# Second layer's attention: query projections in halves, output pieces one by one, each tied behind its step's scores

## The chip, the cores and the metric

The kernel runs on one core of one Trainium2 chip. The metric is the device time of one execution in microseconds (us). Its engines are TensorE (PE in the profile, with PEld for the loading of its weights), VectorE (DVE), ScalarE (ACT), GpSimd (POOL) and SyncE (SP), which here only issues transfers.

## The reference

A trunk of two layers over 512 latent tokens and 256 context tokens, 1024 wide. The change lies in the second layer's first half: grouped-query attention with 16 query heads, 4 key-value heads, head width 64, a window of 128 tokens either way, all context keys, and a learned sink logit per head. Cut to that part:

```python
def mixer_c(h_x, h_c, w_in, w_out, sinks, cos, sin, with_ctx_out):
    q_x, k_x, v_x = jnp.split(h_x @ w_in, [C_Q_COLS, C_Q_COLS + C_KV_COLS], axis=-1)
    q_x = apply_rope(heads(q_x, GQA_HEADS), cos, sin)
    k_x = apply_rope(heads(k_x, GQA_KV_HEADS), cos, sin)
    ...
    def blk(q_b, start):
        ...
        return gqa_sink_attend(q_b, jnp.concatenate([k_c, k_b], axis=1),
                               jnp.concatenate([v_c, v_b], axis=1),
                               jnp.concatenate([ctx_mask, band], axis=-1), sinks)
    out_x = block_sweep(blk, q_x).reshape(B, S, C_Q_COLS) @ w_out
```

Behind it come the gated residual, a norm, the feed-forward and the final norm.

## The kernel before

All arithmetic is in 32 bits. A projection splits both operands into a high and a low part and adds three products of them (`mm3`, L205 to L209: high by high, high by low, low by high), so a tile of 128 output columns by 512 tokens over 1024 inputs is 8 x 3 = 24 matmuls. Weights come through a stream `S`: SP loads a raw tile, ACT casts its high part (L158), DVE subtracts to get the low part (L159); `S.next()` hands out the next pair and makes two more ready ahead. The pools hold three of each.

The attention stage has eight query tiles `m` of two heads each. `q_piece(m)` projects one tile (24 matmuls into PSUM, tile `t` for the first and the single bank `lin` for the others) and calls `q_tile`: the rope (DVE shuffle L380 and product L381, which read the PSUM bank, then two POOL instructions L382 and L383), then ACT (L369) and DVE (L372) write the two halves of `gq`, of which there are four buffers.

There are 32 attention steps, `gqa_step(m, i)`, four per tile, one for each block of 128 queries. Each has two parts. Part `a` makes, for each of two heads, the scores in one of two PSUM buffers `s` (L1513 for the context keys, L1515 for the window; eight matmuls a step), adds the mask and takes the maximum on DVE (L1517), the exponential on ACT (L1522, L1524), the sum and reciprocal on DVE (L1526, L1527) and the scaling on POOL (L1530). Part `b` turns the probabilities by PE transposes (L1542, eight, and L1554, two in the steps with a longer window), copies them out on ACT and DVE (L1550, L1548, L1555), and in every second step makes the value products (L396, a block of twenty matmuls for two steps) and splits the result (L196, L197).

`run_steps` writes the steps out as: part `a` of step n, part `b` of step n - 1, then the fillers of step n. Fillers are projections for PE to do while a softmax is under way. A table `plan` gives them by tile: tiles 1 and 2 of the queries in tile 0's four steps, 3 and 4 in the next four, then one tile for each four steps, and from tile 5 on the eight pieces of `first_part`, the output projection's first half (`wo1` with `k0 = 0`: 12 matmuls over the heads of tiles 0 to 3, into `lin`, and a gated residual on DVE, L1591). The order written is not the order on the engines: a scheduler places each engine's instructions by its own estimate of when their inputs are ready, so it may draw fillers ahead of the step they were written in. Only `issue_after(x)` holds an instruction behind `x`, where both are on one engine.

Behind the 32 steps, the output projection's second half runs (`wo1` with `k0 = 4`), then the residual's norm and the feed-forward.

Of the kernel before, what the change touches and what calls it, by code (L numbers as in the profile page):

```python
# [15 lines left out]
P = 128  # L16
D = 1024
KT = D // P
NX = 512
NC = 256  # L20
# [17 lines left out]
def tile_trunk(  # L38
# [27 lines left out]
    nc = tc.nc  # L66
# [126 lines left out]
    S = Stream()  # L193
# [8 lines left out]
        nc.gpsimd.dma_start(f32(lo), src, accum_op=ALU.add)  # L202
        nc.scalar.copy(hi, src)

    def mm3(ps, wh, wl, xh, xl, n=KT):  # L205
        for k in range(n):
            nc.tensor.matmul(ps, wh(k), xh(k), start=k == 0, stop=False)  # L207
            nc.tensor.matmul(ps, wh(k), xl(k), start=False, stop=False)  # L208
            end = nc.tensor.matmul(ps, wl(k), xh(k), start=False, stop=k == n - 1)  # L209
        return end  # L210
# [17 lines left out]
    def wslice(t, m=P):  # L228
        v = t.rearrange("p (k m) -> p k m", m=m)
        return lambda k: v[:, k, :]  # L230
# [127 lines left out]
    xh = lambda k: hx[k][:, 0, :]  # L358
    xl = lambda k: hx[k][:, 1, :]
# [4 lines left out]
    def evac_pair(dst, col, n, src, scale):  # L364

        c = slice(col, col + n)
        for j in range(2):
            a = slice(64 * j, 64 * j + 64)
            nc.scalar.activation(dst[a, j, c], src[a, :], AF.Copy, scale=scale)  # L369
        for j in range(2):  # L370
            a, o = slice(64 * j, 64 * j + 64), slice(64 - 64 * j, 128 - 64 * j)
            nc.vector.scalar_tensor_tensor(  # L372
                dst[o, j, c], src[a, :], scale, f32(dst[a, j, c]), op0=ALU.mult, op1=ALU.subtract
            )
# [46 lines left out]
    def vload():  # L421
        return [tuple(wslice(t, 256) for t in S.next()) for _ in range(2)]

    def run_steps(steps, fillers):

        prev = None
        for n, (a, b) in enumerate(steps):
            a()
            if prev:
                prev()  # L430
            prev = b
            for f in fillers[n] if n < len(fillers) else []:
                f()
        prev()

    def spread(items, n):
        out_ = [[] for _ in range(n)]
        for i, f in enumerate(items):
            out_[i * n // len(items)].append(f)
        return out_  # L440
# [172 lines left out]
    with ExitStack() as st:  # L613
# [3 lines left out]
        linp = lambda: lin.tile([P, NX], F32, tag="lin", name="lin")  # L617
# [32 lines left out]
        with ExitStack() as s0:  # L650
# [7 lines left out]
            def ada0_mm(b):  # L658
                ps = tp()
                for k in range(KT):  # L660
                    ada_mm(ps, S.next(0), k, k == 0, k == KT - 1)
                    S.request(min(S.at + 8, 2 * KT + 3))
                return ps
# [8 lines left out]
            ps = ada0_mm(0)  # L672
# [381 lines left out]
        ps = linp().rearrange("p (t c) -> p t c", t=2)  # L1054
# [47 lines left out]
        def first_part(t):  # L1102
            def f():
                w = S.next()
                for m in (2 * t, 2 * t + 1):
                    wo_chunk(m, w, "x", 0)
                    wo_chunk(m, w, "c", 0)
            return f

        steps, fillers = [], []  # L1110
        for u in range(8):
# [23 lines left out]
            steps += us  # L1135
            fillers += spread(fl, len(us))
        run_steps(steps, fillers)
        prep(KT - 1)()


        held = []
        for t in range(4):
            w = S.next(3)
# [29 lines left out]
    with ExitStack() as st:  # L1173
# [17 lines left out]
        q_tile = lambda: fp.tile([P, 4 * H], F32, tag="q", name="q")  # L1191
# [234 lines left out]
    with ExitStack() as st:  # L1426
# [6 lines left out]
        linp = lambda: lin.tile([P, NX], F32, tag="lin", name="lin")  # L1433
# [11 lines left out]
        def q_tile(m, ps):  # L1445
            qs[m] = gp.tile([P, 2, NX], F32R, tag="gq", name="gq", bufs=4)
            evac_pair(qs[m], 0, NX, rope_of(ps, gp), -0.125)
# [33 lines left out]
        def q_piece(m):  # L1481
            def f():
                wh, wl = (wslice(t) for t in S.next())
                ps = linp() if m else tp()
                mm3(ps, wh, wl, xh, xl)
                q_tile(m, ps)
            return f

        def att(m):

            if m < 4:
                return hc[2 * m], hc[2 * m + 1]
            return [hx[m][:, i, :].rearrange("p (a n) -> p a n", a=2) for i in range(2)]
# [4 lines left out]
        def gqa_step(m, i):  # L1498
            kv = m // 2
            lo, hi = max(i - 1, 0), min(i + 1, 3)  # L1500
            nk = (hi - lo + 1) * P
            d = {}

            def a():
                q = qs[m]
                small = lambda name: gp.tile([P, 2], F32, tag=name, name=name, bufs=4)
                mx, rs, es = small("mx"), small("rs"), small("es")
                pp = []
                for c in range(2):
                    ql = q[:, c, i * P : (i + 1) * P]  # L1510
                    s = sps.tile([P, 1024], F32, tag="s", name="s")
                    for n, k in ((0, k1), (1, k2)):
                        nc.tensor.matmul(s[:, 256:512], ql, k[:, kv, 0:NC], start=(n == 0), stop=(n == 1))  # L1513
                    for n, k in ((0, k1), (1, k2)):
                        nc.tensor.matmul(s[:, 512 : 512 + nk], ql, k[:, kv, NC + lo * P : NC + lo * P + nk], start=(n == 0), stop=(n == 1))  # L1515
                    sv = s[:, 256 : 512 + nk]
                    nc.vector.tensor_tensor_reduce(  # L1517
                        out=sv, in0=sv, in1=gm0 if i == 0 else gm[:, 0 : 256 + nk], op0=ALU.add, op1=ALU.min,
                        scale=1.0, scalar=snk[:, 2 * m + c : 2 * m + c + 1], accum_out=mx[:, c : c + 1],
                    )  # L1520
                    p = gp.tile([P, 640], F32, tag="p", name="p", bufs=5)
                    nc.scalar.activation(p[:, 0 : 256 + nk], sv, AF.Exp, bias=mx[:, c : c + 1], scale=-1.0, accum_out=rs[:, c : c + 1])  # L1522
                    sk = 2 * m + c
                    nc.scalar.activation(es[:, c : c + 1], snk[:, sk : sk + 1], AF.Exp, bias=mx[:, c : c + 1], scale=-1.0)  # L1524
                    pp.append(p)
                nc.vector.tensor_add(rs, rs, es)  # L1526
                nc.vector.reciprocal(rs, rs)  # L1527
                for c in range(2):
                    z = pp[c][:, 0 : 256 + nk]
                    nc.gpsimd.tensor_scalar(z, z, rs[:, c : c + 1], 1.0, op0=ALU.mult, op1=ALU.mult)  # L1530
                d["p"] = pp
# [71 lines left out]
        for m in range(KT):  # L1603
# [2 lines left out]
        super_weights(1, type("", (), {"tile": lambda self, *a, **k: spool[0].tile(*a, **k)})())  # L1606
        q_piece(0)()
        steps, fillers = [], []
        plan = {
            0: [q_piece(1), q_piece(2)], 1: [q_piece(3), q_piece(4)], 2: [q_piece(5)], 3: [q_piece(6)], 4: [q_piece(7)],  # L1610
            5: first_part(0), 6: first_part(1) + first_part(2), 7: first_part(3),
        }
        for m in range(8):
            steps += [gqa_step(m, i) for i in range(4)]
            fillers += spread(plan[m], 4)
        run_steps(steps, fillers)
        held = []
        for t in range(4):
            w = S.next(0 if t >= 2 else 2)
# [336 lines left out]
```

## Time and profile before

| what | us |
|---|---|
| median of three runs | 1614.59 (1612.83 to 1619.76) |
| the profiled execution | 1613.67 |
| its span in the profile | 1611.6 |
| PE busy | 1538.8 (95%) |
| DVE busy | 1252.2 (78%) |
| ACT busy | 743.4 (46%) |
| POOL busy | 273.5 (17%) |
| first scores of the stage | at 1047.00 |
| last value products begin | at 1219.27 |

The span is counted from the profile's first instruction to its last; the execution's own time has 2.1 us around it. All places are given in us from the span's start. Matmuls overlap, so the time from the start of one to the start of the next is what one costs in a row, and not its own duration. PE being busy is no proof that it runs at full clock; the windows give the clock that was granted, 1.00 being full.

### The profile page before, as it was taken

Reading aid. Unit: us, or ns where it says so; the run is one execution under the profiler, and the core shown is the slowest. Engines: PE = TensorE matmul, PEld = TensorE weight load, DVE = VectorE, ACT = ScalarE, POOL = GpSimd, SP = SyncE. Lnnn points to the kernel's source line nnn. Section 1 sums busy time; section 2 is a strip of 40 time slices with the busy share of each in tenths; the row PEclk is TensorE's granted clock in tenths of the full one; section 3 lists DMA queues with packets and bytes.
Section 4 is the critical chain, followed back from the end, with each engine's and each line's share of the span. In section 5 each row is a group of like instructions: output and inputs, shape, how many; then the busy total and the mean of one; then the engine's idle time right before and its main releaser. Section 6 shows DMA issues by size and latency. Waiting matters only on the chain.

```text
span 1611.6 us, 25394 instructions
## 1 busy us (share of the span) xinstructions
PE 1538.8 (95%) x9774; PEld 1378.4 (86%) x9774; DVE 1252.2 (78%) x2141; ACT 743.4 (46%) x1292; POOL 273.5 (17%) x311
## 2 busy tenths in 40 slices
PE   5899999998999999999999999998999999999997
PEld 3798988787878999999999998886778899989897
DVE  4757789876698889869899777686766987868686
ACT  5445655455344523333424245466764543525344
POOL 2222214354010000010100001264332000000001
PEclk9999999999999999999999999999999999999999
DMA  9322255544145455575756752311011441323321
GB/s 347 103 62 77 78 160 163 180 152 117 57 144 144 119 165 155 150 197 159 206 171 164 211 155 83 107 56 38 14 40 46 138 144 66 131 68 104 118 79 53
DMA packets 69216, 198.41 MB, mean 123 GB/s; under 512 B 6900, under 2 KB 19348, under 8 KB 69096
## 3 DMA queue, kind: packets, MB, share of 16 engines
q1 hardware_dynamic: 59464, 164.40, 31.0%
q0 software_dynamic: 9056, 31.87, 9.4%
q8 instruction: 77, 1.26, 0.3%
q10 hardware_dynamic: 576, 0.52, 0.1%
q14 instruction: 43, 0.35, 0.1%
HBM read 160.45 MB, written 4.86 MB: 103 GB/s over the span
## 4 chain that ended last, share of the span: by engine, by line
PE 49%; DVE 10%; DMA 6%; issue 4%; ACT 1%; POOL 0%; DVEq 0%; POOLq 0%; ACTq 0%; SPq 0%
PE f L1737 4%; PE f L1736 4%; PE f L1735 4%; DMA wl<-raw 3%; PE f L208 3%; PE f L209 3%; PE f L207 3%; PE f L1307 2%; PE f L1305 2%; PE f L1306 2%; PE f L1788 2%; PE f L1789 2%; PE f L1790 2%; PE t L396 2%; DMA raw<-in_w_dram 2%
## 5 line engine op out<-in xcount | busy, mean ns | idle before, releaser
L196 ACT ACTIVATE wh<-raw 128x1024 fp32r<-128x1024 f32 (+1 forms) x96 | 92.2, 978 | 232.2 <-DVE raw L525 102.2
L207 PE MATMUL lin<-hb,wh 128*128 128x512 f32 (+1 forms) x456 | 161.6, 356 | 9.9 <-DVE k L372 4.2
L208 PE MATMUL lin<-hb,wh 128*128 128x512 f32 (+1 forms) x456 | 159.8, 351 | 0.2
L209 PE MATMUL lin<-hb,wl 128*128 128x512 f32 (+1 forms) x456 | 158.3, 347 | 0.0
L197 DVE TENSOR_TENSOR wl<-raw,wh 128x1024 fp32r<-128x1024 f32 (+1 forms) x96 | 107.2, 1122 | 36.4 <-ACT wh L196 34.5
L269 DVE SCALAR_TENSOR_TENSOR junk<-raw,tables 128x1024 bf16<-128x1024 f32 x80 | 98.9, 1237 | 19.0 <-DMA raw<-in_ada_wT_dram 18.6
L202 POOL DMA_DIRECT2D wl<-raw x39 | 34.1, 874 | 445.2 <-ACT wl L201 346.0
L207 PEld LDWEIGHTS lin<-hb,wh 128*128 128x128 f32 x456 | 86.5, 190 | 24.0 <-issue 5.7
L1346 PE MATMUL f<-g,wh 128*128 128x512 f32 (+1 forms) x304 | 102.8, 339 | 0.5 <-DVE s L1335 0.5
L1347 PE MATMUL f<-g,wh 128*128 128x512 f32 (+1 forms) x304 | 102.7, 339 | 0.0
L1736 PE MATMUL f<-hb,wh 128*128 128x256 f32 x360 | 101.7, 283 | 0.0
L1348 PE MATMUL f<-g,wl 128*128 128x256 f32 (+1 forms) x304 | 100.8, 336 | 0.9 <-DMA wl<-raw 0.9
L1735 PE MATMUL f<-hb,wh 128*128 128x256 f32 x360 | 101.4, 283 | 0.0
L1737 PE MATMUL f<-hb,wl 128*128 128x256 f32 x360 | 101.2, 283 | 0.0
L208 PEld LDWEIGHTS lin<-hb,wh 128*128 128x128 f32 x456 | 86.7, 190 | 11.4 <-issue 0.6
L1307 PE MATMUL f<-hb,wl 128*128 128x384 f32 x288 | 96.2, 334 | 0.0
L1305 PE MATMUL f<-hb,wh 128*128 128x384 f32 x288 | 96.2, 334 | 0.0
L1306 PE MATMUL f<-hb,wh 128*128 128x384 f32 x288 | 96.2, 334 | 0.0
L209 PEld LDWEIGHTS lin<-hb,wl 128*128 128x128 f32 x456 | 86.6, 190 | 10.7
L158 ACT CAST wh<-raw 128x1024 fp32r<-128x1024 f32 x61 | 63.9, 1047 | 66.6 <-PE lin L208 17.6
L159 DVE TENSOR_TENSOR wl<-raw,wh 128x1024 fp32r<-128x1024 f32 x61 | 79.1, 1297 | 18.0 <-ACT wh L158 17.6
L339 POOL TENSOR_TENSOR ns_a<-ns_a,ns_s 128x256 f32<-128x256 f32 (+1 forms) x16 | 18.7, 1169 | 430.9 <-ACT ns_s L335 424.3
(393 smaller groups left out, 4883.1 us busy)
## 6 DMA issues: line engine op xcount, KB each, us to landing
raw<-in_w_dram SPq DMA_DIRECT2D x132, 512.0 KB, 3.7
raw<-in_ada_wT_dram SPq DMA_DIRECT2D x80, 512.0 KB, 4.1
wl<-raw POOLq DMA_DIRECT2D x39, 512.0 KB, 6.5
raw<-in_w_ab_dram SPq DMA_DIRECT2D x24, 512.0 KB, 3.9
raw<-in_ada_w_dram SPq DMA_DIRECT2D x16, 512.0 KB, 9.4
k<-k SPq DMA_DIRECT2D x16, 384.0 KB, 5.1
raw<-in_w_c_dram SPq DMA_DIRECT2D x12, 512.0 KB, 3.9
nb<-in_na_bias_dram POOLq DMA_DIRECT2D x16, 256.0 KB, 3.4
```

The costliest lines, as they stand in the source:

```text
L197: return nc.vector.tensor_sub(lo, src, f32(hi))
L207: nc.tensor.matmul(ps, wh(k), xh(k), start=k == 0, stop=False)
L208: nc.tensor.matmul(ps, wh(k), xl(k), start=False, stop=False)
L209: end = nc.tensor.matmul(ps, wl(k), xh(k), start=False, stop=k == n - 1)
L1305: nc.tensor.matmul(ps, wh(k), b[:, 0, :], start=k == 0, stop=False)
L1306: nc.tensor.matmul(ps, wh(k), b[:, 1, :], start=False, stop=False)
L1307: nc.tensor.matmul(ps, wl(k), b[:, 0, :], start=False, stop=k == 3)
L1346: nc.tensor.matmul(ps, hi, g[:, 0, cols[v]], start=first, stop=False)
L1347: nc.tensor.matmul(ps, hi, g[:, 1, cols[v]], start=False, stop=False)
L1735: nc.tensor.matmul(ps, wh(k), b[:, 0, :], start=k == 0, stop=False)
L1736: nc.tensor.matmul(ps, wh(k), b[:, 1, :], start=False, stop=False)
L1737: nc.tensor.matmul(ps, wl(k), b[:, 0, :], start=False, stop=k == 3)
```

## The change

`q_piece` stays for tile 0 alone. Tiles 1 to 7 are projected by `q_halves(m)`: two fillers of 12 matmuls, the first over the inputs 0 to 3, the second over 4 to 7 into the same `lin` bank, with the rope behind the second. The table is gone. The 14 halves are spread over steps 0 to 16 (none in steps 5, 11 and 16), the eight output pieces over steps 17 to 31 (steps 17, 18, 20, 22, 24, 26, 28, 30). And each step's fillers are written inside `issue_after` on the last score matmul issued, `scored[0]`, which is that of the same step: a filler can no longer be drawn ahead of its step's scores.

```diff
-    def mm3(ps, wh, wl, xh, xl, n=KT):
-        for k in range(n):
+    def mm3(ps, wh, wl, xh, xl, n=KT, ks=None):
+        for k in ks or range(n):
...
-    def run_steps(steps, fillers):
+    def run_steps(steps, fillers, pin=None):
...
-            for f in fillers[n] if n < len(fillers) else []:
-                f()
+            with tc.issue_after(pin[0].ins) if pin else nullcontext():
+                for f in fillers[n] if n < len(fillers) else []:
+                    f()
...
+        def q_halves(m):
+            d = {}
+
+            def f(i):
+                if i == 0:
+                    d["w"] = [wslice(t) for t in S.next()]
+                    d["ps"] = linp()
+                mm3(d["ps"], *d["w"], xh, xl, ks=range(4 * i, 4 * i + 4))
+                if i:
+                    q_tile(m, d["ps"])
+
+            return [lambda i=i: f(i) for i in range(2)]
+
+
+        scored = [None]
+
...
-                        nc.tensor.matmul(s[:, 512 : 512 + nk], ql, k[:, kv, NC + lo * P : NC + lo * P + nk], start=(n == 0), stop=(n == 1))
+                        scored[0] = nc.tensor.matmul(s[:, 512 : 512 + nk], ql, k[:, kv, NC + lo * P : NC + lo * P + nk], start=(n == 0), stop=(n == 1))
...
-        plan = {
-            0: [q_piece(1), q_piece(2)], 1: [q_piece(3), q_piece(4)], 2: [q_piece(5)], 3: [q_piece(6)], 4: [q_piece(7)],
-            5: first_part(0), 6: first_part(1) + first_part(2), 7: first_part(3),
-        }
         for m in range(8):
             steps += [gqa_step(m, i) for i in range(4)]
-            fillers += spread(plan[m], 4)
-        run_steps(steps, fillers)
+
+        fillers = spread([f for m in range(1, 8) for f in q_halves(m)], 17) + spread([f for t in range(4) for f in first_part(t)], 15)
+        run_steps(steps, fillers, scored)
```

The order of PE, DVE, ACT and POOL differs only inside this stage; SP's does not differ. In the changed kernel the lines stand a little lower: the scores are L1530 and L1532 there, DVE's mask L1534, the transposes L1559 and L1571, the copies L1565, the sums L1543 and L1544.

**PE ahead of the first scores.** Before, the end of tile 0's projection (into `t`) is followed by tile 1's, into `lin`:

```order
L208 MATMUL t<-hb_131,wh 128x512
L209 MATMUL t<-hb_131,wl 128x512
L207 MATMUL lin<-hb_124,wh 128x512
L208 MATMUL lin<-hb_124,wh 128x512
L209 MATMUL lin<-hb_124,wl 128x512
L207 MATMUL lin<-hb_125,wh 128x512
```

Now the scores of step 0 follow at once, and tile 1's first half stands behind them:

```order
L208 MATMUL t<-hb_131,wh 128x512
L209 MATMUL t<-hb_131,wl 128x512
L1530 MATMUL s<-gk_9404,gq 128x256
L1530 MATMUL s<-gk_9405,gq 128x256
L1532 MATMUL s<-gk_9404,gq 128x256
L1532 MATMUL s<-gk_9405,gq 128x256
L1530 MATMUL s<-gk_9404,gq 128x256
L1530 MATMUL s<-gk_9405,gq 128x256
L1532 MATMUL s<-gk_9404,gq 128x256
L1532 MATMUL s<-gk_9405,gq 128x256
L207 MATMUL lin<-hb_124,wh 128x512
```

All 24 matmuls of tile 1 have moved from before the first scores to behind them, 12 behind step 0's and 12 behind step 1's.

**PE near the end of the stage.** Before, the last steps stand with no filler between them (`t<-ident,p` are transposes, `t<-pt,gv` value products):

```order
L1542 MATMUL t<-ident,p 128x128 x8
L1554 MATMUL t<-ident,p 128x128 x2
L1513 MATMUL s<-gk_9404,gq 128x256
L1513 MATMUL s<-gk_9405,gq 128x256
L1515 MATMUL s<-gk_9404,gq 128x256
L1515 MATMUL s<-gk_9405,gq 128x256
L396 MATMUL t<-pt,gv 64x256 x6
L396 MATMUL t<-pt,gv 64x128 x2
L396 MATMUL t<-pt,gv 64x256 x2
L1513 MATMUL s<-gk_9404,gq 128x256
```

Now an output piece stands behind every second step's scores, up to the last but one:

```order
L1559 MATMUL t<-ident,p 128x128 x8
L1530 MATMUL s<-gk_9404,gq 128x256
L1530 MATMUL s<-gk_9405,gq 128x256
L1532 MATMUL s<-gk_9404,gq 128x384
L1532 MATMUL s<-gk_9405,gq 128x384
L207 MATMUL lin<-hb_124,wh 128x512
L208 MATMUL lin<-hb_125,wh 128x512
L209 MATMUL lin<-hb_124,wl 128x512
```

The last piece of before stands ahead of six steps' scores that have none; after, only the last step's scores have none behind them.

**DVE at a rope.** Before, tile 1's rope stands on DVE ahead of all scores of step 0 (`rt` and `ru` are the rope's tiles):

```order
L372 SCALAR_TENSOR_TENSOR gq<-rt,gq 64x512 x2
L380 STREAM_SHUFFLE ru<-lin 128x512
L381 TENSOR_TENSOR rt<-lin,tables 128x512
L1517 ISA s,mx<-s,gm_9401,snk 128x512
L1517 ISA mx 128x1
L159 TENSOR_TENSOR wl<-raw,wh 128x1024
```

Now it stands behind those of steps 0 and 1 and ahead of step 2's:

```order
L1543 TENSOR_TENSOR rs<-rs,es 128x2
L1565 COPY pt<-t 128x2x256
L1544 RECIPROCAL rs<-rs 128x2
L380 STREAM_SHUFFLE ru<-lin 128x512
L381 TENSOR_TENSOR rt<-lin,tables 128x512
L1534 ISA s,mx<-s,gm,snk 128x640
L1534 ISA mx 128x1
```

The rope's two reads have moved from before the stage's first score work into the run of the softmax, and the next tile's first half waits for them, since it writes the same `lin` bank.

## Prediction

> **What bounds the kernel now.** I read the page first, for the span:
>
> ```profile
> span 1611.6 us, 25394 instructions
> ```
>
> Then, because the change touches only the second layer's attention, I cut that stage with the view of windows. The cuts lie at the starts of the blocks of value products (L396), of which there is one for every two steps. The columns after the window's length are busy us of PE, PEld, DVE, ACT and POOL (with instruction counts), the granted clock, the DMA share and GB/s.
>
> ```profile
> core 0: us, PE busy (x) PEld busy (x) DVE busy (x) ACT busy (x) POOL busy (x), PEclk, DMA share, GB/s
> 1047.00:1071.16 24.16, 23.39 (x120) 19.27 (x122) 20.41 (x40) 15.01 (x31) 13.63 (x11) 1.00 0.21 72
> 1071.16:1088.11 16.95, 16.95 (x104) 13.99 (x106) 14.15 (x29) 10.07 (x26) 11.17 (x10) 1.00 0.15 38
> 1088.11:1101.12 13.01, 13.00 (x82) 10.08 (x84) 7.82 (x17) 5.81 (x16) 5.75 (x6) 1.00 0.21 73
> 1101.12:1114.75 13.63, 9.68 (x63) 7.00 (x64) 9.88 (x24) 8.64 (x22) 6.07 (x6) 1.00 0.13 39
> 1114.75:1129.69 14.94, 13.73 (x107) 10.55 (x107) 11.43 (x30) 10.99 (x30) 4.54 (x6) 1.00 0.01 2
> 1129.69:1144.47 14.78, 14.06 (x112) 11.18 (x112) 12.45 (x33) 12.15 (x35) 6.31 (x8) 1.00 0.01 2
> 1154.36:1189.93 35.57, 35.57 (x237) 29.11 (x238) 24.29 (x53) 20.07 (x52) 11.47 (x12) 1.00 0.15 45
> 1189.93:1219.27 29.34, 25.35 (x201) 19.21 (x201) 19.96 (x52) 19.57 (x53) 11.27 (x14) 1.00 0.06 20
> ```
>
> TensorE is full where projections are mixed in (1071 to 1101, 1154 to 1190) and has holes where they are not (1101 to 1114, and after 1190). The timeline of PE says what those holes wait for; the bracket is the idle time before the row and what ended it:
>
> ```profile
> 1108.38 0.50 PE L1513 MATMUL s<-gk,gq 128*128 128x256 f32 x2 [1.33 <-ACT p L1522]
> 1112.64 1.32 PE L1542 MATMUL t<-ident,p 128*128 128x128 f32 x8 [1.39 <-POOL p L1530]
> 1196.13 0.50 PE L1513 MATMUL s<-gk,gq 128*128 128x256 f32 x2 [0.81 <-ACT p L1522]
> 1203.03 0.50 PE L1513 MATMUL s<-gk,gq 128*128 128x256 f32 x2 [0.88 <-ACT p L1522]
> 1219.27 1.09 PE L396 MATMUL t<-pt,gv 128*64 128x256 f32 x10 [0.88 <-DVE pt L1548]
> ```
>
> So an unfilled step waits on its own softmax: the next scores need one of two score buffers, which the exponential (L1522) must have read. The last row is the end of the stage, where nothing is left to fill with.
>
> How much is lost? A full stretch gives the price of a step. The chain of waits has these blocks:
>
> ```profile
> 1154.36 2.10 PE t L396 x20
> ...
> 1166.22 2.10 PE t L396 x20
> ...
> 1178.07 2.10 PE t L396 x20
> ...
> 1189.93 2.10 PE t L396 x20
> ```
>
> They are 11.86 us apart, each time two steps and 24 projection matmuls. Those matmuls follow one another at 0.227 us (the first two rows of the next fence, 0.68 us for three). Two steps alone are thus 11.86 - 24 x 0.2275 = 6.40 us: **3.20 us a step**. The stage runs from the first scores at 1047.00 to the end of the last block, 1219.27 + 2.10 = 1221.37: 174.4 us. By the order, it holds 32 steps and 240 projection matmuls: 32 x 3.20 + 240 x 0.2275 = 157.0 us. So 17.4 us are lost in it. By stretch, with the order's count of matmuls taken off: 1101 to 1114 loses 13.63 - 6 x 0.2275 - 6.40 = 5.9; 1114 to 1144 (eight steps, six matmuls) loses 2.8; from 1190 on at least 29.34 - 8 x 3.20 = 3.7, of which the last row's 0.88 us is an end that any order has; the rest lies before 1101.
>
> **Part 1: the fill is laid evenly (a gain).** After has 14 halves of 12 matmuls over steps 0 to 16 and eight output pieces of 12 over steps 17 to 31. In the last 15 steps its order repeats one pattern, each score group behind a block of values, transposes or projection, as in the full stretch of before. I therefore price these at 3.20 with nothing lost. The waits of 5.9, 2.8 and 2.8 us (3.7 without the end) go: 11.5 us.
>
> In the first 17 steps the full stretches of before are the nearest rows: 16.95 - 44 x 0.2275 - 6.40 = 0.54 us lost on two steps, and 13.01 - 25 x 0.2275 - 6.40 = 0.92. That is 0.27 to 0.46 a step; I take the middle, 0.365 x 17 = 6.2 us. The bounds are 0 (the stretch after 1154) and the 5.9 us per two steps of 1101 to 1114, which the DVE rival below takes up. What brings a loss here is the single bank of the projections (`lin`): five tiles start their first half in the step after the last tile's second half, so PE waits until DVE's two rope reads (L380 and L381) are through.
>
> **Part 2: the tie empties PE ahead of the first scores (a loss).** Before, 24 matmuls of tile 1 stand on PE between tile 0 and the first scores; after, they are tied behind those scores. The rope of tile 0 is a chain over four engines (timeline of PE, chain of waits, timeline of PE):
>
> ```profile
> 1040.24 0.39 PE L207 MATMUL t<-hb,wh 128*128 128x512 f32 x1
> ...
> 1040.92 0.39 PE L207 MATMUL lin<-hb,wh 128*128 128x512 f32 x1
> ...
> 1041.16 0.76 DVE ru L380
> ...
> 1042.05 1.30 POOL ru L382
> ...
> 1043.42 2.16 POOL rt L383
> 1045.60 0.64 ACT gq L369
> 1046.26 0.68 DVE gq L372
> ...
> 1047.00 0.50 PE L1513 MATMUL s<-gk,gq 128*128 128x256 f32 x2 [0.48 <-DVE gq L372]
> ```
>
> Tile 0 leaves PE at about 1041.1 and the scores start at 1047.00. Before hides this under 24 x 0.2275 = 5.5 us of work. After leaves PE empty for 5.9 us; the chain has the same instructions in the same order, so I keep 1047.00. Those 5.5 us are then done inside the stage, which holds 264 matmuls: 32 x 3.20 + 264 x 0.2275 = 102.4 + 60.1 = 162.5 us.
>
> The hole also costs clock. This trace has two places with PE idle as long (timeline of PE, then windows of 2 us):
>
> ```profile
> 311.54 0.47 PE L207 MATMUL lin<-hb,wh 128*128 128x512 f32 x1 [3.17 <-DVE k L372]
> ...
> 312.72 0.63 PE L208 MATMUL lin<-hb,wh 128*128 128x512 f32 x1
> ...
> 372.54 0.55 PE L937 MATMUL s<-k,q 128*128 128x256 f32 x1 [4.21 <-DMA k<-k]
> ```
>
> ```profile
> 312.00:314.00 2.00, 2.00 (x7) 1.53 (x6) 1.97 (x6) 0.00 (x0) 0.00 (x0) 0.58 0.00 0
> 314.00:316.00 2.00, 2.00 (x7) 1.57 (x6) 1.97 (x5) 0.00 (x0) 0.00 (x0) 0.57 0.68 231
> 316.00:318.00 2.00, 2.00 (x10) 1.46 (x8) 1.92 (x5) 0.00 (x0) 0.00 (x0) 1.00 0.60 217
> ...
> 372.00:374.00 2.00, 1.46 (x7) 1.49 (x8) 0.34 (x1) 0.00 (x0) 0.00 (x0) 0.50 0.07 24
> 374.00:376.00 2.00, 2.00 (x11) 2.00 (x10) 1.10 (x3) 1.53 (x4) 0.00 (x0) 0.50 0.00 0
> 376.00:378.00 2.00, 1.73 (x9) 1.25 (x7) 1.79 (x4) 1.33 (x5) 0.58 (x1) 0.71 0.67 203
> ```
>
> Behind the gap of 3.17 us the clock is short by 0.42 x 2 + 0.43 x 2 = 1.7 us of work; behind that of 4.21 by 0.50 x 1.46 (PE began at 372.54) + 0.50 x 2 + 0.29 x 2 = 2.3 us. I take 1.8, nearer the lower one: the first scores, and the projection behind them, are what runs slowly. The bounds are 0 (softmax hides it) and 2.3. The Trainium skill (TensorE: Matmul & The Clock Gate, "What's actually happening") halves the clock after an idle window of about 3.4 us and gives it back after a busy one, which speaks against this change; by one such window at half rate the term would be an estimated 1.7 us, and the sum 0.1 us lower. The trace has the clock down behind a gap of 3.17 us already, so here the measurement is the stricter of the two.
>
> **Part 3: the other queues.** The tie is an order on PE alone; it adds no semaphore. What stands behind a waiting first score on PE is all of tile 1. On SP the list of loads is the same, so transfers keep their turn. The cast of a weight (L158 on ACT, L159 on DVE) comes later by some steps because tiles free later, but two weights are ready ahead, and in the output projection that follows both orders have the same rows. On POOL the rope's two instructions move behind more of the softmax scalings; tiles 1 to 7 are ready by steps 1, 3, 6, 8, 10, 13 and 15 and needed at 4 to 28. I cost these at nothing; without that lead a late tile would show 3.6 us of POOL work (1.30 + 2.16) as a wait.
>
> **Sum.** 162.5 + 6.2 (first 17 steps) + 0.9 (end) + 1.8 (clock) = 171.4 us against 174.4: 3.0 us saved. The profiled execution took 1613.67 us, which would become 1610.7. The median of the three runs is 1614.59, 0.92 us above that execution, so I forecast 1611.6 us. A measurement of this kernel tells about 0.5%, 8.1 us, from no change; the forecast lies within it.
>
> **Rivals.**
> - *Dense everywhere.* If the first 17 steps lose nothing, as after 1154, and the softmax of step 0 hides the clock, 6.2 + 1.8 us more are saved: 11.0 us, 1603.6. For it: half as much fill per step as in 1047 to 1101, so fewer ropes crowd a step. Against it: one `lin` bank. Chance 0.12.
> - *DVE sets the pace of the first 17 steps.* Its work there is estimated from these rows and the windows:
>
> ```profile
> 1048.36 0.70 DVE rt L381
> ...
> 1109.57 1.22 DVE L159 TENSOR_TENSOR wl<-raw,wh 128x1024 fp32r<-128x1024 f32 x1
> ...
> 1234.33 0.50 DVE res L1591
> ```
>
> The stretch of 35.57 us has 24.29 us of DVE for six steps, three casts and three residuals: (24.29 - 3 x 1.22 - 3 x 0.50) / 6 = 3.19 us a step. A tile costs 0.76 + 0.70 + 2 x 0.68 + 1.22 = 4.04. Seventeen steps and seven tiles make 82.5 us, in a front that I put at 17 x 3.20 + 14 x 2.73 + 6.2 = 98.8 us: a share of 0.84. Two stretches with PE full ran at 20.41 / 24.16 = 0.84 and 14.15 / 16.95 = 0.83. But the stretch 1101 to 1114 reached only 9.88 / 13.63 = 0.72, its instructions standing in a bad order. At that share the front takes 82.5 / 0.725 = 113.8 us, 15.0 more: 12.0 slower than before, 1626.6. It decides below a share of 82.5 / (98.8 + 11.1) = 0.75. Chance 0.15.
> - *The gain is given back behind the stage.* If the weights of the feed-forward arrive by a clock of their own, an earlier end only waits for them: 1614.6. For it, the DMA share where they are loaded, 0.65 with PE not full:
>
> ```profile
> 1240.00:1260.00 20.00, 17.14 (x120) 15.20 (x119) 19.75 (x45) 12.39 (x26) 2.31 (x2) 1.00 0.65 211
> ```
>
> Against it: 0.65 is not full, and DVE, at 19.75 of 20 us, carries the norm on which PE waits there; that work follows the stage's end and moves with it. Chance 0.10.
>
> **How the numbers follow.** The forecast's own case (0.2 to 0.6 us lost a step, 1607.5 to 1615.5) has 0.63. Faster by over 0.5% needs nearly all of the dense case: 0.12. Slower by over 0.5% needs the DVE case: 0.15. The rest, 0.73, is within 0.5%. The range runs from 1605 (most of the dense case) to 1620 (half way into the DVE case, which leaves about 0.1 above).
>
> **What would show it.** In the trace of after: PE idle for 5 to 6 us ahead of the first scores, ended by DVE's L372, and a granted clock near 0.5 in the 3 to 4 us behind; the value blocks of the last 15 steps at two steps plus one piece, 6.40 + 2.73 = 9.1 us; few waits of scores on ACT; 171 us from first scores to the last value block. The forecast is wrong if the first scores come well before 1047, if the clock stays at 1.00 there, if the front takes over 105 us or under 94, or if the output projection waits for a weight.

## The result and the profile after

| | before | after |
|---|---|---|
| median us | 1615.54 (19 runs, 1611.55 to 1619.76) | 1621.31 (19 runs, 1618.50 to 1627.24) |
| ratio after / before | | 1.0042, 95% interval 1.0032 to 1.0052 |
| span of the profiled execution, us | 1611.6 | 1621.2 |
| mean granted clock | 0.994 | 0.988 |

The changed kernel is slower, by 0.42%. That is within the 0.5% that the prediction called no change, but the interval lies clear of 1, the forecast saving of 3 us became a loss of 5.8 us, and 1621.3 lies 1.3 us above the range.

First, the whole stage, first scores to the end of the last value products, in the windows of each kernel, before and then after. The columns are the length, busy us of PE, PEld, DVE, ACT and POOL with counts, granted clock, DMA share, GB/s.

```profile
1047.00:1221.37 174.37, 163.72 (x1105) 129.96 (x1105) 127.47 (x294) 109.81 (x280) 74.74 (x78) 1.00 0.11 35
```

```profile
1048.24:1231.00 182.76, 172.69 (x1128) 139.67 (x1128) 129.31 (x294) 109.54 (x280) 72.67 (x78) 0.96 0.11 34
```

The stage became 8.4 us longer. PE's idle time hardly changed: 174.37 - 163.72 = 10.65 us before, 182.76 - 172.69 = 10.07 after. What grew is PE's busy time, by 9.0 us: 24 matmuls moved in (5.5 us), and the other 3.5 us stand beside a clock that fell from 1.00 to 0.96. So the idle time moved to other places, and behind these the clock was low. The start is 1.24 us later, for reasons ahead of the stage (it lies between 1043 and 1052 in the profiles of this study), and 8.4 + 1.2 is the whole difference of the spans: behind the stage nothing was won or lost.

Where it sits, by stretch, in the windows of after. The cuts are again at blocks of value products:

```profile
1048.24:1078.88 30.64, 29.53 (x164) 24.46 (x165) 22.34 (x51) 17.83 (x45) 12.80 (x12) 0.92 0.12 41
1078.88:1112.09 33.21, 33.14 (x223) 27.16 (x223) 26.98 (x59) 21.73 (x55) 18.34 (x19) 1.00 0.10 33
1112.09:1133.00 20.91, 18.07 (x100) 14.51 (x102) 15.24 (x32) 10.44 (x27) 9.27 (x8) 0.92 0.13 35
1133.00:1149.82 16.82, 14.70 (x110) 11.26 (x112) 13.16 (x26) 12.02 (x30) 8.75 (x8) 0.97 0.16 53
1149.82:1164.02 14.20, 14.20 (x88) 11.54 (x90) 8.34 (x22) 7.80 (x20) 4.51 (x6) 0.92 0.00 1
1173.01:1191.72 18.71, 18.31 (x133) 15.26 (x133) 13.17 (x34) 12.35 (x34) 5.87 (x8) 1.00 0.08 29
1191.72:1210.42 18.70, 18.30 (x133) 15.26 (x133) 13.17 (x34) 12.35 (x34) 5.88 (x8) 1.00 0.10 30
1219.63:1227.24 7.61, 4.87 (x38) 3.13 (x39) 4.04 (x10) 3.52 (x10) 1.36 (x2) 1.00 0.23 71
1227.24:1232.00 4.76, 4.76 (x24) 3.17 (x25) 0.42 (x1) 0.38 (x1) 0.00 (x0) 0.64 0.00 0
```

Three places have a clock below 1.00: the start, 1112 to 1164, and the end. Between them PE is full or nearly so, at full clock. The timeline of PE in after names the waits at these places:

```profile
1048.24 0.80 PE L1530 MATMUL s<-gk,gq 128*128 128x256 f32 x2 [5.85 <-DVE gq L372]
...
1118.37 0.80 PE L1530 MATMUL s<-gk,gq 128*128 128x256 f32 x2 [1.61 <-ACT p L1539]
...
1148.54 0.64 PE L1530 MATMUL s<-gk,gq 128*128 128x256 f32 x2 [2.12 <-ACT p L1539]
...
1225.04 1.32 PE L1559 MATMUL t<-ident,p 128*128 128x128 f32 x8 [1.01 <-POOL p L1547]
1227.24 3.83 PE L396 MATMUL t<-pt,gv 128*64 128x256 f32 x20 [0.88 <-DVE pt L1565]
```

The first is the gap that the prediction named. The second and third stand at an *empty* step (a step without filler; they are steps 5, 11 and 16) directly behind the rope of a query tile: tile 5's second half is in step 10, tile 7's in step 15. I call these two the knots. Step 5, which follows a first half and so no rope, has no such wait. The last two are the end.

How a knot is made is to be seen around 1112 on three engines of after: DVE, ACT and POOL, in this order, from their timelines.

```profile
1111.86 2.29 DVE L159 TENSOR_TENSOR wl<-raw,wh 128x1024 fp32r<-128x1024 f32 x1
1114.07 0.75 DVE L1534 CUSTOM_DVE_ANT_0 s<-s,gm,snk 128x512 f32<-128x512 f32 x1
```

```profile
1114.97 0.69 ACT L1539 ACTIVATE p<-s,mx 128x512 f32<-128x512 f32 x1 [3.01 <-DVE mx L1534]
...
1115.83 1.27 ACT L369 ACTIVATE gq<-rt 64x512 fp32r<-64x512 f32 x2
...
1117.54 0.69 ACT L1539 ACTIVATE p<-s,mx 128x512 f32<-128x512 f32 x1
```

```profile
1111.79 1.28 POOL L382 TENSOR_TENSOR ru<-ru,tables 128x512 f32<-128x512 f32 x1
1113.15 2.14 POOL L383 TENSOR_TENSOR rt<-rt,ru 128x512 f32<-128x512 f32 x1
```

The empty step's scores start on PE at 1110.61 and 1111.31. Their masks (L1534) wait on DVE behind the cast of the next weight (L159), which takes 2.29 us beside POOL's rope. The first exponential (L1539) can start only at 1114.97. Between it and the second one stands the finished rope's write into `gq` (L369, 1.27 us). PE has neither filler nor scores to go on with, and waits 0.52 and then 1.61 us. In a filled step the same queue costs next to nothing (the six steps from 1078.88 to 1112.09, which hold 60 projection matmuls, lose 0.4 us), because up to 2.7 us of projection lie on PE meanwhile. The clock follows at both knots (windows of after):

```profile
1116.00:1118.00 2.00, 0.76 (x6) 0.52 (x5) 1.55 (x5) 1.93 (x4) 0.00 (x0) 1.00 0.46 184
1118.00:1120.00 2.00, 1.63 (x6) 1.53 (x7) 1.52 (x4) 2.00 (x8) 0.00 (x0) 0.51 0.00 0
1120.00:1122.00 2.00, 2.00 (x8) 1.56 (x7) 0.99 (x4) 1.07 (x4) 1.33 (x2) 0.64 0.00 0
...
1148.00:1150.00 2.00, 1.46 (x6) 1.03 (x8) 0.73 (x3) 1.52 (x6) 0.00 (x0) 0.69 0.00 0
1150.00:1152.00 2.00, 2.00 (x14) 1.24 (x14) 1.09 (x4) 1.05 (x3) 0.67 (x1) 0.50 0.00 0
```

At the first, PE was busy for 0.76 of 2 us, and the next 4 us ran at 0.51 and 0.64 of the clock.

### The profile page after: what moved, and what is told of

It reads as the page before. It is cut to its first block, busy times and chain, and to the rows that moved or that the text cites. A ratio compares the mean times of both kernels' runs of the same rounds, so it can differ in the third digit from the quotient of the medians.

```text
span 1621.2 us, 25360 instructions
## 1 busy us (share of the span) xinstructions
PE 1542.7 (95%) x9774; PEld 1384.8 (85%) x9774; DVE 1253.8 (77%) x2141; ACT 742.7 (46%) x1292; POOL 269.7 (17%) x311
## 3 DMA queue, kind: packets, MB, share of 16 engines
q8 instruction: 77, 1.26, 0.3%
## 5 line engine op out<-in xcount | busy, mean ns | idle before, releaser
L269 DVE SCALAR_TENSOR_TENSOR junk<-raw,tables 128x1024 bf16<-128x1024 f32 x80 | 98.8, 1235 | 19.8 <-DMA raw<-in_ada_wT_dram 19.4
L159 DVE TENSOR_TENSOR wl<-raw,wh 128x1024 fp32r<-128x1024 f32 x61 | 80.5, 1319 | 18.0 <-ACT wh L158 17.9
```

The source lines that it names most:

```text
L269: nc.vector.scalar_tensor_tensor(junk, raw, 1.0, cs[0], op0=ALU.mult, op1=ALU.mult, accum_out=col[:, 0])
```

## The experiments

Theory A: three places lose, each idle time and clock: the start, which the tie empties; the empty steps behind a rope; and the last step, whose piece is laid in step 30 so that step 31 is bare. Its first rival is the prediction's: DVE has too much to do in the first 17 steps, whatever their order, and sets their pace. A later rival puts the knots down to the weight casts on DVE alone. Each kernel is after with the edit shown. A stage is that of the one profiled execution (182.8 us in after, 174.4 in before); ratios are to before, with 95% intervals. Each ratio is good to 0.0010 to 0.0014 either way (e4's to 0.0022), so two of them differ clear of noise when they are some 0.0015 to 0.0017 apart: under about 1.0025, a kernel is less slow than after, whose ratio is 1.0042. A stage of one execution says less by itself, because the clock can fall in one execution and not in another (e1).

### e1_untied: the laying without the tie

```diff
-        run_steps(steps, fillers, scored)
+        run_steps(steps, fillers)
```

> The even laying without the tie. The order differs from the changed kernel in the first two steps alone: tile 1's 24 matmuls stand ahead of the first scores again; from step 2 on every row is the same. Theory A (the tie costs the empty stretch ahead of the first scores and the clock behind it, and the two later stalls have nothing to do with it): 5.5 us of matmuls and 1.5 to 2 us of clock come back, about 1614 us, PE idle under 1 us ahead of the first scores, the long waits of scores in steps 9 to 14 still there. Rival B (VectorE and ScalarE set the pace of the first 17 steps, so a head start of TensorE is waited away): 1619 to 1621 us, with the later waits longer.

Measured: 1615.48 us, ratio 1.000 (0.9986 to 1.0014), stage 174.4. The windows row of its stage:

```profile
1049.21:1223.58 174.37, 165.09 (x1105) 131.10 (x1105) 127.57 (x294) 109.72 (x280) 74.53 (x78) 0.99 0.11 35
```

The expectation described this kernel wrongly. Its order differs from after's far beyond the first two steps: it is, instruction for instruction on all five engines, the order of the kernel before. Without the tie the scheduler draws the halves back to where it had put whole tiles. So laying the fillers out differently did nothing by itself, the tie does everything, and this run did not tell A from the DVE rival.

It shows something else. At the same rows of the order as in before, PE waits 0.53 and then 1.33 us. Behind them before kept a clock of 1.00, and this execution did not:

```profile
1110.00:1112.00 2.00, 1.41 (x5) 1.01 (x5) 1.97 (x6) 1.31 (x4) 1.28 (x1) 0.62 0.00 0
1112.00:1114.00 2.00, 2.00 (x7) 1.72 (x7) 2.00 (x5) 0.38 (x3) 1.96 (x1) 0.53 0.03 2
```

The next wait, 1.39 us in before, is 0.51 here, and the stages are equal to 0.01 us: a fall of the clock just ahead of another wait cost nothing.

### e2_filled_gap: the empty start filled with idle matmuls

```diff
         q_piece(0)()
+        keep_busy(tp(), 22)
```

> The changed kernel with 22 small matmuls that nobody reads in the empty stretch ahead of the first scores: the stretch stays, only the clock should not fall. Theory A: the granted clock is 1.00 behind the first scores and 1.5 to 2 us come back, about 1619.5 us. Rival B (the softmax of the first steps hides the slow clock): 1621 us with the clock at 1.00.

Measured: 1619.02 us, ratio 1.0024 (1.0014 to 1.0035), stage 181.0. Windows behind its first scores (at 1049.15):

```profile
1049.00:1051.00 2.00, 1.85 (x11) 1.58 (x12) 1.86 (x5) 0.25 (x2) 0.00 (x0) 1.00 0.23 92
1051.00:1053.00 2.00, 2.00 (x11) 1.64 (x10) 0.80 (x4) 1.59 (x6) 0.00 (x0) 1.00 0.00 0
```

The clock stays at 1.00 where after has 0.50, and the stage is 1.8 us shorter: the clock term of the prediction, in its size. The waits at the knots are untouched (0.52, 1.61 and 2.13 us).

### e3_last_step: the last piece in the last step

```diff
+        fillers[31], fillers[30] = fillers[30], []
         run_steps(steps, fillers, scored)
```

> The changed kernel with the last output piece in step 31 and none in step 30. Theory A (the last transposes and value products wait uncovered, and the low activity lowers the clock for the last value block): the waits there shrink from 2.7 us in all to about 1 and the last value block takes 2.1 us and not 3.8, so 2 to 3.5 us come back, about 1618.5 us. Rival B (the wait only moves to step 30, which now has no filler): 1621 us.

Measured: 1619.41 us, ratio 1.0024 (1.0013 to 1.0035), stage 180.2, 2.6 us shorter. Its last value products on PE:

```profile
1227.74 2.17 PE L396 MATMUL t<-pt,gv 128*64 128x256 f32 x20 [0.93 <-DVE pt L1565]
```

They take 2.17 us and not 3.83, at full clock, and the waits ahead are 0.40 and 0.93 in place of 0.84, 1.01 and 0.88. So the end in after is not one that any order has.

### e4_old_plan_tied: the tie with the old table

```diff
-        fillers = spread([f for m in range(1, 8) for f in q_halves(m)], 17) + spread([f for t in range(4) for f in first_part(t)], 15)
+        plan = {
+            0: [q_piece(1), q_piece(2)], 1: [q_piece(3), q_piece(4)], 2: [q_piece(5)], 3: [q_piece(6)], 4: [q_piece(7)],
+            5: first_part(0), 6: first_part(1) + first_part(2), 7: first_part(3),
+        }
+        fillers = [f for m in range(8) for f in spread(plan[m], 4)]
```

> The table of the kernel before (whole tiles, output pieces from tile 5 on) with the tie. Theory A (the tie's cost is the start): the first scores wait 5 to 6 us as in the changed kernel, the pieces can no longer be drawn ahead, so the last steps are filled; about 7 us lost and 4 to 5 won, 1617 to 1619 us. Rival B (the tie costs only together with the halves): 1615 us or less.

Measured: 1644.42 us, ratio 1.0173 (1.0151 to 1.0195), stage 201.0. Both theories missed the size. PE's timeline shows why:

```profile
1146.90 3.47 PE L396 MATMUL t<-pt,gv 128*64 128x256 f32 x20 [2.69 <-ACT gq L369]
...
1171.60 1.73 PE L396 MATMUL t<-pt,gv 128*64 128x256 f32 x16 [2.69 <-ACT gq L369]
```

A whole tile tied to one step leaves up to three empty steps behind each rope, and six waits of 2.0 to 2.7 us stand in the stage, with a clock of 0.94 over it. This is the knot many times over. It also shows that the laying does matter under a tie: with the tie alone the kernel would have lost 1.7%.

### e5_holes_between: the empty steps moved away from the ropes

```diff
+        fillers[11], fillers[10], fillers[16], fillers[15] = fillers[10], [], fillers[15], []
         run_steps(steps, fillers, scored)
```

> The changed kernel with the empty steps 11 and 16 moved: tile 5's second half goes from step 10 to 11 and tile 7's from 15 to 16, so that an empty step lies between a tile's two halves and not behind its rope. Theory A (the long waits of the changed kernel stand where a rope, its casts and copies come ahead of the next steps' masks and exponentials and the next step has no filler to cover that): the waits of 1.6 and 2.1 us of scores and the slow clock behind them go, 5 to 6 us come back, about 1616 us. Rival C (the weight cast on VectorE, slowed to 2 us by the rope's work on GpSimd, costs the same wherever it stands): 1620 to 1622 us.

The same work and the same number of empty steps; they now stand between the two halves of tiles 5 and 7. Measured: 1616.26 us, ratio 1.0014 (1.0002 to 1.0026), stage 178.1, 4.7 us shorter. Windows over the places of the knots, and the wait left there on PE:

```profile
1098.95:1122.80 23.85, 22.42 (x146) 17.24 (x145) 18.06 (x43) 16.19 (x43) 11.43 (x12) 1.00 0.12 41
1122.80:1144.99 22.19, 21.20 (x142) 16.87 (x142) 17.55 (x38) 13.21 (x33) 11.54 (x11) 1.00 0.13 35
```

```profile
1118.41 0.50 PE L1530 MATMUL s<-gk,gq 128*128 128x256 f32 x2 [0.90 <-ACT p L1539]
```

The waits of 1.61 and 2.12 became 0.90 and 0.69 and the clock holds. Of the 4.7 us, about 0.6 come from a clock that was back sooner at the start in this execution. DVE has the same work in the same 17 steps, so its amount is not what limits; the place of the empty step is.

### e6_no_cast: one weight for all tiles

```diff
-        for j in (9, 0, 1, 2, 3, 4, 5, 6, 7):
+        for j in (9, 0):
...
+                w_first[:] = [wh, wl]
...
-                    d["w"] = [wslice(t) for t in S.next()]
+                    d["w"] = w_first
```

> The changed kernel with tiles 1 to 7 projected with tile 0's weights: seven loads and fourteen casts (seven on ScalarE, seven on VectorE) are left out, the ropes stay. Rival C (the casts make the waits): the waits of scores behind steps 10 and 15 go, 5 to 6 us come back, about 1615.5 us. Theory A (rope, copies and casts together, uncovered): half of it comes back, 1618 to 1619 us, and waits of about 1 us stay there.

This kernel leaves out the weights of tiles 1 to 7, with their loads and their casts on ACT and DVE, and projects those tiles with tile 0's. Measured: 1613.38 us, ratio 0.9990 (0.9978 to 1.0002), stage 176.5. Its remaining waits on PE at the start and in the front:

```profile
1051.11 0.79 PE L1533 MATMUL s<-gk,gq 128*128 128x256 f32 x2 [4.98 <-DVE gq L372]
1114.28 2.17 PE L396 MATMUL t<-pt,gv 128*64 128x256 f32 x20 [0.94 <-DVE rs L1547]
```

At the knots no wait is over 0.94 us, the clock there is 1.00, and the stage is 6.3 us shorter. Most of a knot goes with the casts and their loads, which this run does not tell apart; the time is nearer to what rival C said, the waits of about 0.9 us that stay are what theory A said. The start gap is 0.9 us shorter too: there, POOL's rope no longer runs beside a cast (L383 takes 1.26 us and not 2.12).

### e7_ahead_even: tile 1 ahead of the loop, the rest laid evenly

```diff
-        fillers = spread([f for m in range(1, 8) for f in q_halves(m)], 17) + spread([f for t in range(4) for f in first_part(t)], 15)
+        q_piece(1)()
+        fillers = spread([f for m in range(2, 8) for f in q_halves(m)], 17) + spread([f for t in range(4) for f in first_part(t)], 15)
```

> Tile 1 projected whole ahead of the loop, as the kernel before has it on TensorE; the twelve halves of tiles 2 to 7 tied and spread evenly over steps 0 to 16, which leaves empty steps behind the ropes of tiles 5, 6 and 7. Theory A: the 5.5 us of matmuls and about 2 us of clock at the start come back, the waits behind the ropes stay: 1613 to 1615 us. Rival B (VectorE and ScalarE set the pace of the first 17 steps): 1618 us or more.

Measured: 1619.63 us, ratio 1.0032 (1.0019 to 1.0044), stage 178.6: about 5 us above the expectation, and not clear of noise from after. On PE:

```profile
1051.91 0.50 PE L1530 MATMUL s<-gk,gq 128*128 128x256 f32 x2 [0.48 <-DVE gq L372]
...
1059.08 0.51 PE L1530 MATMUL s<-gk,gq 128*128 128x256 f32 x2 [1.47 <-ACT p L1539]
1071.10 2.17 PE L396 MATMUL t<-pt,gv 128*64 128x256 f32 x20 [1.54 <-DVE pt L1565]
...
1131.89 0.50 PE L1530 MATMUL s<-gk,gq 128*128 128x256 f32 x2 [1.67 <-ACT p L1539]
...
1151.20 0.50 PE L1530 MATMUL s<-gk,gq 128*128 128x256 f32 x2 [1.77 <-ACT p L1539]
```

The start is cured, and 24 matmuls have left the stage. But twelve halves over 17 steps leave five empty steps, three of them behind a rope, with waits of 1.00, 1.67 and 1.77 us there. The two waits of about 1.5 us early in the loop are another matter: e8 has them too. I had counted the start's gain and neither of these.

### e8_ahead_holes_last: tile 1 ahead, no empty step behind a rope, a piece in the last step

```diff
+        q_piece(1)()
+        fillers = [[] for _ in range(17)] + spread([f for t in range(4) for f in first_part(t)], 15)
+        for m, at in zip(range(2, 8), ((0, 1), (2, 4), (5, 7), (8, 10), (11, 13), (14, 16))):
+            for n, f in zip(at, q_halves(m)):
+                fillers[n] = [f]
+        fillers[31], fillers[30] = fillers[30], []
```

> All three places at once: tile 1 ahead of the loop, the empty steps of tiles 2 to 7 laid between a tile's halves, the last output piece in step 31. Theory A: 7.5 + 5.5 + 2 us less than the changed kernel, about 1606.5 us, 0.5% under the kernel before, with PE idle under 4 us in the stage. Rival B: 1614 us or more.

Measured: 1610.28 us, ratio 0.9978 (0.9967 to 0.9989), stage 172.0 at a clock of 1.00: faster than both kernels, but not the 1606.5 I wrote, and PE idles for 172.02 - 162.73 = 9.3 us in the stage, not under 4. The two longest waits that stayed on PE, early in the loop:

```profile
1050.51 0.50 PE L1530 MATMUL s<-gk,gq 128*128 128x256 f32 x2 [1.47 <-ACT p L1539]
...
1062.53 2.17 PE L396 MATMUL t<-pt,gv 128*64 128x256 f32 x20 [1.56 <-DVE pt L1565]
```

Ahead of the first, ACT waits 1.26 us for POOL's L383 in tile 1's rope, writes `gq` (L369, 1.28 us), and only then comes to the exponential, which starts at 1049.67: tile 1's rope, once more ahead of the scores, now stands in the first softmax.

### e9_rope_on_dve: after, with the rope's last two operations on DVE

```diff
-        nc.gpsimd.tensor_mul(u, u, sint)
-        nc.gpsimd.tensor_add(t, t, u)
+        eng.tensor_mul(u, u, sint)
+        eng.tensor_add(t, t, u)
```

`eng` is DVE for the query tiles of this stage.

> The changed kernel with the two products of a query tile's rope on VectorE in place of GpSimd. Theory C (VectorE and GpSimd hold one another up: a cast takes 1.22 us alone and about 2.1 beside a rope, a rope's last sum 1.29 alone and 2.15 beside a cast): casts at 1.2 us everywhere, the empty stretch at the start shorter by about 2 us, the waits behind steps 10 and 15 under 1 us, about 1615 us. Theory A without C (it is the amount of rope work ahead of the next masks, of which VectorE now has 1.3 us more a tile): the start gains 2 us, the waits stay, about 1619 us.

Measured: 1617.74 us, ratio 1.0021 (1.0007 to 1.0035), stage 177.9: between what the theories said. Two rows of it, the cast (DVE) at the first knot and the wait (PE) at the second:

```profile
1110.62 1.23 DVE L159 TENSOR_TENSOR wl<-raw,wh 128x1024 fp32r<-128x1024 f32 x1
```

```profile
1143.59 0.50 PE L1530 MATMUL s<-gk,gq 128*128 128x256 f32 x2 [1.35 <-ACT p L1539]
```

No cast of a query tile's weight is slowed any more, and the start gap is 5.30 us; waits of 1.73 and 1.35 us remain at the knots. Theory C's 2 us at the start came to 0.55. So the slowing by POOL looks like a part of a knot and the order of the work like the rest; the run also gives DVE more to do, and does not divide them.

### e10_all_rope_on_dve: e8 and e9 together

> The same in the kernel with all three places mended (tile 1 ahead, empty steps between halves, last piece in the last step), which took 1610.3 us. Theory C: the waits of 1.5 us at 1050 and 1062 go, 2 to 4 us less, about 1607.5 us. Theory A without C: VectorE's 1.3 us more a tile show where the steps are filled, 1611 to 1613 us.

Measured: 1605.61 us, ratio 0.9948 (0.9935 to 0.9962), the fastest of the study. The windows row over its stage, which opens 0.91 us ahead of the first scores (they start at 1047.91, so the stage is 167.5 us), and the page's line:

```profile
1047.00:1215.40 168.40, 162.53 (x1110) 131.20 (x1108) 133.68 (x309) 110.05 (x282) 51.94 (x64) 1.00 0.12 38
```

```profile
span 1605.5 us, 25376 instructions
```

The waits of 1.47 and 1.56 us of e8 are gone. PE idles for 5.9 us in this window, against 9.3 in e8's stage and 10.1 in after's, while DVE has more to do (133.68 us against 128.64 and 129.31): the opposite of what a pace set by DVE would give.

### e11_holes_last: e5 and e3 together, the tied start kept

> The changed kernel with the empty steps between a tile's halves and the last piece in step 31, tied from the first step on as it was. If the places add up: 182.8 us of stage less 4.7 and 2.6, about 175.5 us from the first scores to the end of the last value block, 1614.4 us, and what is left over the kernel before is the empty stretch at the start. If they do not: 177 to 178 us, 1616 us.

Measured: 1615.08 us, ratio 0.9998 (0.9988 to 1.0009).

```profile
1048.53:1223.22 174.69, 168.27 (x1128) 136.23 (x1128) 129.17 (x294) 108.59 (x280) 74.75 (x78) 0.99 0.11 35
```

The stage is 174.7 us, 8.1 less than after's, where e5 and e3 alone took off 4.7 and 2.6 (7.3): the two places add up. What is left, the tied start (5.85 us of wait, then half clock), uses up what the rest of the laying wins, and the kernel is level with before. From here to e8 the median falls by 4.8 us (1615.08 to 1610.28): that is what tile 1 ahead of the loop was worth, with its rope in the first softmax and tiles 2 to 7 laid in other steps.

## Why the prediction failed

*The start: right.* The gap is 5.85 us (5 to 6 forecast), ended by L372, and 24 matmuls moved into the stage. The granted clock in windows of after behind it:

```profile
1048.24:1050.00 1.76, 1.76 (x8) 1.76 (x9) 1.16 (x2) 0.00 (x0) 0.00 (x0) 0.50 0.26 107
1050.00:1052.00 2.00, 2.00 (x7) 1.62 (x7) 1.14 (x4) 1.65 (x6) 0.00 (x0) 0.50 0.00 0
1052.00:1054.00 2.00, 2.00 (x8) 1.58 (x7) 0.33 (x2) 0.17 (x1) 1.27 (x2) 0.71 0.00 0
```

That is 0.50 x 1.76 + 0.50 x 2 + 0.29 x 2 = 2.5 us of clock. The term was 1.8, and e2 gave 1.8 back. (The prediction writes POOL's 1.30 + 2.16 us as 3.6; they are 3.46, and nothing was worked out from them.)

*The last 15 steps: right.* Four steps and two pieces took 18.7 us (18.2 forecast), and from 1164 to 1219.6 only 0.8 us was lost. The waits of before did go, up to the end.

*The first 17 steps: wrong, and the main failure.* The step was "the full stretches of before are the nearest rows", 0.365 us lost a step. With the order's count of 36, 12 and 24 matmuls, the stretches from 1112 to 1164 lose 20.91 - 8.19 - 6.40 = 6.3, 16.82 - 2.73 - 12.80 = 1.3 and 14.20 - 5.46 - 6.40 = 2.3: 9.9 us over eight steps, against 2.9 forecast, 7.0 too little. The six steps ahead of them lost only 33.21 - 60 x 0.2275 - 19.2 = 0.4. So the price per step was no rate at all: two knots hold it, and e5 made the stage 4.7 us shorter by moving two empty steps. Nor did the wait that the prediction named come: it had PE wait for the rope's reads (L381) before the next tile's first half, and no wait that PE's timeline shows in this stage ends there; those of the knots end at exponentials (L1539). An average from full stretches can't price an empty step; the row to use was before's own unfilled stretch (5.9 us on two steps), which the prediction kept for the DVE rival.

*The other queues: wrong in part.* The prediction asked only whether weights and tiles arrive in time, and they did. It did not ask what a cast, the rope and the writes of `gq` delay on DVE and ACT: the masks and exponentials of an empty step. e6 shows that most of the loss goes without the casts and their loads, too.

*The end: wrong.* The term was 0.9 us, "an end that any order has". The rows from the last block but one to the last took 1231.00 - 1219.63 = 11.37 us; in before the same rows are

```profile
1213.75:1221.37 7.62, 6.72 (x59) 4.59 (x59) 2.95 (x7) 3.41 (x10) 2.95 (x4) 1.00 0.01 2
```

7.62 us, so 3.75 more, of which e3 gives 2.6 back by one piece laid a step later.

*The sum.* 7.0 (eight steps), 3.75 (end) and 0.8 (last steps) are 11.55 us, and the miss is 182.8 - 171.4 = 11.4. What is left for the first nine steps and the clock at the start is -0.15: they took about the 5.1 us that the prediction gave them. That is a remainder and was not measured by itself, and the cut at 1164 has half a step's scores more ahead of it than the one at 1112, about 0.6 us. Read another way: the clock, costed only at the start at 1.8 us, was short by 0.04 x 182.76 = 7.3 us of work over the stage. Not all of that need have been lost: PE's busy time grew by only 3.5 us beyond the added matmuls. How much of the miss is clock therefore stays open, but it came behind waits for which the prediction had put down no clock.

*The sign that should have caught it did not.* Step 17's first scores start at 1148.54, 100.3 us after the first ones, inside the 94 to 105 that the prediction set. But scores run ahead of value products: by then three steps of these (1.5 blocks of 2.17 us) and a step of transposes (1.04 us) were still owed, so the cut left work out that the 98.8 us held. With it the front took about 104.6 us, which still would not have crossed the bound of 105: the bound was also too wide. The signs that did show it were the waits of scores on ACT, which should have been few, and the 171 us of the stage.

*The rivals.* A general pace set by DVE fell (e5, e10); the piece of it that held is that the order of DVE's work, in one bad spot, decides. "Given back behind the stage" was not put to the test by after, whose stage ends later. It fell with e10: the last value products end at 1215.4 there and at 1221.4 in before, and the spans are 6.1 us apart (1605.5 and 1611.6). "Dense everywhere" fell at the knots.

*What stays open.* How the knots divide between the casts and their loads, the slowing of a cast by POOL and the place of `gq` on ACT: e6 and e9 overlap. What decides whether the clock falls behind a wait. And the stages are of one profiled execution each: after's is 8.4 us longer than before's, while the medians differ by 5.8.

## What to carry to other kernels

Filler that is tied to a step cannot be drawn to where a wait opens, so under a tie the empty steps have to be placed by hand: between the halves of a projection and not behind its end, where the rope, the next weight's cast and the result's write queue up on the softmax's engines; and one filler belongs in the last step. Before tying anything behind the first scores, keep there the work that covers the chain into them (here one whole tile). And price waits on PE with the clock that they may take from what follows; here that was up to about 1.6 us of work at a knot, in some executions and not in others.

## What was unexpected of the hardware

**The clock falls behind short waits, and not behind all of them.** A wait of 1.61 us, with another of 0.52 less than 3 us ahead of it, was followed by 4 us at 0.51 and 0.64; the one of 2.12 us by 4 us at 0.69 and 0.50; at the end, waits of 0.84, 1.01 and 0.88 us within 4.5 us took the last value products to 3.83 us from 2.17. But waits of 1.73 us in e9 and 1.77 us in e7 left the clock at 1.00, and so did nearly the same three waits at the end of e7 (0.84, 1.02, 0.87). Of the two waits of 2.69 us shown in e4, the first was followed by 0.54 and 0.60, the second by 1.00. And e1, with before's order and waits of 0.53 and 1.33 us at the same place, lost clock where before did not. So neither the length of a wait nor the order of the work decides it alone. The Trainium skill (TensorE: Matmul & The Clock Gate, "What's actually happening") gives an idle window of about 3.4 us for the drop; here it came with no PE wait over 1.33 us (e1), so the measurement decides. The same section of the Trainium skill says that this window runs freely, which could be why like waits differ; no run here tests that.

**A cast on DVE and the rope on POOL take turns.** The cast takes 1.21 to 1.23 us alone and up to 2.29 beside the rope; L383 takes 1.29 alone and 2.14 beside the cast. At the first knot POOL's L382 runs from 1111.79 for 1.28 us, unslowed; the cast "starts" at 1111.86 and ends at 1114.15, 1.08 us after L382's end; L383 "starts" at 1113.15 and ends at 1115.29, 1.14 after the cast's end. Each thus looks as if it had waited for the other's whole instruction and then run at about its own pace. That agrees with the Trainium skill (SBUF — State Buffer, "SBUF: two separate sides"), by which DVE and GpSimd share a pair of ports as an exclusive lock and not as a division of the bandwidth, when the DVE instruction has two inputs in SBUF, as the cast has, and GpSimd reads SBUF too. DVE's masks, whose scores lie in PSUM, took 0.75 us beside the same L383, as they do elsewhere. If the cast does wait, the busy time of DVE and POOL holds waiting. In e9, fourteen instructions more on DVE, of about 0.68 us each, cost it only 132.36 - 129.31 = 3.05 us of busy time over the stage, while the casts of the query tiles' weights took 1.20 to 1.23 us:

```profile
1048.15:1226.04 177.89, 169.92 (x1128) 137.28 (x1128) 132.36 (x308) 108.59 (x280) 53.84 (x64) 0.97 0.11 35
```
